# The opening of a two-layer trunk: c spread by products over 128 lines, factors by way of DRAM, a later half of weights and a sum in halves

## The chip, the cores and the metric

The kernel runs on one core of a Trainium2 chip. The metric is the device time of one execution, in microseconds (us); the time of a version is the median of its runs. A core has five engines with a queue of instructions each: TensorE (PE; its weight loads are shown apart as PEld), VectorE (DVE), ScalarE (ACT), GpSimd (POOL) and SyncE (SP), which here only issues DMAs. Each queue is worked off in order; an instruction waits until what it reads is there and the buffer that it writes is free. Transfers are moved by 16 DMA engines, whichever engine issues them. A "line" of a tile is one of its 128 partitions.

## The reference, cut to what matters

Two layers, 512 tokens of width 2048, all in float32. The modulation of a layer is three vectors of 2048 (shift, scale, gate), from a vector c. Layer 0 is a chunked retention, layer 1 a latent attention; the change lies in the opening of layer 0, up to its first projection.

```
c_act = silu(c)
for i in range(2):
    shift, scale, gate = split(c_act @ ada_w[i] + ada_b[i], 3)
    h = rmsnorm(x, norm_g[i]) * (1 + scale) + shift        # 512 x 2048
    proj = h @ w_in                                        # layer 0: q, k, v, gate
    y = retention(q, k, v) or attention(...)
    x = x + gate * (silu(g) * norm(y)) @ w_out
return rmsnorm(x, final_norm_g)
```

## The kernel before

Everything is kept transposed: features on the 128 lines, the 512 tokens along a line. The 2048 features are 16 blocks kt of 128; two blocks make a unit u. Each engine's order is the order of the program text: `queued(f)` puts what f issues behind whatever stands last on ACT, DVE, PE and SP; `behind(e)` does so for the engine named. No planner reorders it. Tiles of one tag share a fixed number of buffers, so a load into a recycled buffer waits for the last reader of the tile before.

A float32 product is made from two parts of each operand: a high part, rounded (a cast on ACT, L397), and the rest, the low part (a subtraction on DVE, L398 for weights, L485 for hT). Each product then takes three passes: high by high, one of the mixed ones ("early"), and the other mixed one ("late").

The opening runs like this:

- Loads on SP: x (eight parts), then in turn rows of ada_t ("aw(kt,s)", 1 MB each, s = 0 for shift, 1 for scale; `load_mod`, some in two halves) and 512 columns each of the first weights v, g and qk by units (`first_load`, 512 KB a unit). Four buffers hold aw, three the weights of later units.
- c comes as one line. Four products of one line of `ones` with it spread it to 128 lines in PSUM (`c_ps`), and ACT's silu writes it back as `c_all`. A transposition puts 48 rows of small vectors (biases, gains) into columns (`vec_ps`), which DVE copies to `vcol`.
- For each of the four blocks t of 128 tokens, ACT and DVE sum the squares of x, and POOL raises them to the power -1/2 (`x_r`, called `norm[t]` in the code). DVE (ACT for the last) multiplies the identity by it: `x_diag`. Products of x with the diagonal transpose and scale x at once into `xT_ps`; ACT copies them to `xT` (`keep_x`). Four more products of `ones` with the diagonals (`x_r` in PSUM) spread the factors to all lines, and DVE copies them to `x_factors`, with which the units u > 3, whose x^T is loaded later, are normalised on DVE (L716).
- POOL writes a line of `c_all` to DRAM (`c_d`) for later.
- The modulation of block kt: DVE multiplies aw(kt,s) by c_all and sums along the line (`sum_mod`, L425, one instruction of 2048 elements, or two of 1024). ACT makes the columns b_col and a_col of it (L453, L463), then hT_kt = a_col * xT + b_col as high part (L479), and again in full as h_3f or the like (L484), from which DVE makes the low part.
- PE takes, for each kt, the products of hT_kt with the weights v, g or qk that have a bank of PSUM at that time. For kt = 2 and 3 these are qk and g (the eight early passes of qk, its four late ones, then g), then v for u = 1, and so on. `prepare_ahead(2, low, ...)` writes the work of unit 2 between.

The names below: g_1 are the weights g of unit 1 (kt = 2, 3), whose two halves of 512 elements a line belong to kt = 2 and kt = 3; low hT_3 is the subtraction for hT_3 at L485; "sum (4,0)" is `sum_mod(4, 0)`.

Of the kernel before, what the change touches and what calls it, by code (L numbers as in the profile page):

```python
# [16 lines left out]
P = 128  # L17
# [32 lines left out]
def hybrid_trunk_kernel(  # L50
# [42 lines left out]
    o2_d = dram.tile([D, T], F32, name="o2_d")  # L93
    c_d = dram.tile([1, D], F32, name="c_d")

    def big(name, dt=F32R):
# [278 lines left out]
    def first_load(kind, u):  # L375

        cn = 512
        where = (("k4b", 4), ("k4b", 4)) if kind == "g" else None
        raw = big(f"{kind}0_{u}_raw", F32) if u == 0 else base.tile(
            [P, 2, cn], F32, tag="raw", bufs=3, name=f"{kind}0_{u}_raw"  # L380
        )
        src = w_first[u, "vgq".index(kind[0])]
        if u == 0:
            full[kind] = raw

        def load(*ki):
            if u < 4:
                nc.sync.dma_start(raw[:, ki[0]] if ki else raw, src[:, ki[0]] if ki else src)
            else:
                with behind(mybir.EngineType.Pool):  # L390
                    POOL.dma_start(raw, src)

        def prepare(*ki):
            if (kind, u) not in loaded:
                loaded[kind, u] = two_tiles(where, [P, 2, cn], f"{kind}0_{u}_p")
            hi, lo, w = (t[:, ki[0]] if ki else t for t in (*loaded[kind, u], raw))
            ACT.copy(hi, w)  # L397
            return lambda: DVE.tensor_sub(lo, w, hi.bitcast(F32))  # L398

        if kind == "qk" or u > 0:  # L400
            load()
        prepare.load = load
        return prepare

    def load_mod(kt, s):

        aw = l0p.tile([P, D], F32, tag="aw", bufs=4, name=f"aw_{kt}_{s}")
        n = 2 if kt < 2 or (kt, s) == (2, 0) else 1
        for j in range(n):
# [130 lines left out]
    def queued(fn, *args):  # L540
        with behind(A_, V_, T_, S_):
            return fn(*args)
# [77 lines left out]
    c_all = l0p.tile([P, D], F32, name="c_all")  # L620
    queued(ACT.dma_start, c_all[0:1, :], c)
    vrow = tmp("vec_rows", (P, P))
# [6 lines left out]
    for j, ps in enumerate(c_ps):  # L629
        queued(PE.matmul, ps, ones[0:1, :], c_all[0:1, j * T : (j + 1) * T], True, True)  # L630
        if j == 2:
            queued(PE.transpose, vec_ps[:, :N_OPEN], vrow[:N_OPEN, :], ident[:N_OPEN, :N_OPEN])

    def silu(j):
# [77 lines left out]

    factors = tmp("x_factors")

    def normalise(u):
        DVE.tensor_mul(xT[u], xT[u], factors.unsqueeze(1).to_broadcast([P, 2, T]))  # L716

    def load_unit(u):
# [11 lines left out]
        if u == 1:  # L730
            load_first("g", u)
        if u > 1:
            load_first(there, u)
        mods[2 * u + 1, 1] = queued(load_mod, 2 * u + 1, 1)
        if u == 1:
            load_first(there, u)
# [4 lines left out]
    def prepare_ahead(u, first=None, between=lambda: None):  # L741


        here, there = ("v", "qk") if u % 2 == 0 else ("qk", "v")
        low = queued(prepares[here, u])
        if u < 4:
            queued(first)
        queued(sum_mod, 2 * u, 0)
        if u > 3:
# [27 lines left out]
    for kt in (4, 5):  # L777
        keep_x(kt)
    x_r = acc("x_r")
    for t in range(NT):  # L780
        queued(PE.matmul, x_r[:, t * P : (t + 1) * P], ones, diags[t], True, True)
    queued(sum_mod, 0, 1, 0)
# [6 lines left out]
    queued(low_v)  # L789
    queued(DVE.tensor_copy, factors, x_r)  # L790
    queued(sum_mod, 1, 0, 0)
# [33 lines left out]
    queued(low)  # L825
    lows = [queued(prepares["g", 1], i) for i in range(2)]
    queued(lows[0])
    queued(sum_mod, 3, 1)
    low = make_first(3)
    queued(lows[1])  # L830
    queued(low)
    late[1] = queued(prepares["v", 1])
    queued(late[1])
    low = lambda: None
# [1954 lines left out]
```

## Time and profile before

| | |
|---|---|
| median of 3 runs | 2030.03 us (2029.43 to 2030.13) |
| the profiled execution | 2030.33 us |
| its span in the trace | 2028.5 us |
| TensorE busy | 2014.1 us, 99% of the span |
| VectorE busy | 1661.2 us, 82% |
| ScalarE busy | 1068.3 us, 53% |
| bytes moved by DMA | 462.44 MB, mean 228 GB/s |

The page's shares are means over the whole span; the change touches the first 62 us of it, so the parts that follow read the trace in stretches. Times of rows are in us from the start of the span. The names of tiles stand without their buffer numbers there: `aw<-aw,c_all` is a sum_mod, `g_p` a prepared g, `pair` a prepared tile of v or qk of the first units.

### The profile page before, as it was taken

The page shows a single profiled execution, that of the slowest core. Times are in us where ns is not written, and L with a number is a line of the kernel's source. Part 1 is how long each engine was busy: PE and PEld are TensorE (multiplying, and loading weights), DVE is VectorE, ACT ScalarE, POOL GpSimd, SP SyncE. Part 2 cuts the span into 40 slices and gives each one's busy share as a digit, 9 for nine tenths or more (in the row PEclk, how much of TensorE's full clock was granted, in tenths as well). Part 3 has the DMA queues.
Part 4 walks back from the last instruction along what each step waited for, and adds up shares of the span by engine and source line. Part 5 has one row for each costly group of instructions (what it writes and reads, how often), then busy time and mean ns, then how long its engine had stood idle before and what let it go on. Part 6 is the DMA issues. An engine that isn't in the chain of part 4 may idle for free.

```text
span 2028.5 us, 30162 instructions
## 1 busy us (share of the span) xinstructions
PE 2014.1 (99%) x11105; PEld 1806.9 (89%) x11105; DVE 1661.2 (82%) x2490; ACT 1068.3 (53%) x1697; POOL 109.7 (5%) x188
## 2 busy tenths in 40 slices
PE   9999999999999999999999999999999999999998
PEld 6888898989999888888888888899889999999888
DVE  7999888888989889776888788778978788886765
ACT  6777444544444544434444545445446676775444
POOL 0011010000000000000000000010001000000000
PEclk9999999999999999999999999999999999999999
DMA  9976787878787778765757576763467644446744
GB/s 386 416 304 228 237 281 234 286 229 276 253 268 262 240 248 296 264 207 188 248 177 263 181 252 212 272 203 108 165 198 217 198 145 150 124 149 221 240 151 142
DMA packets 225174, 462.44 MB, mean 228 GB/s; under 512 B 20785, under 2 KB 80241, under 8 KB 221569
## 3 DMA queue, kind: packets, MB, share of 16 engines
q1 hardware_dynamic: 210592, 414.25, 61.6%
q0 software_dynamic: 13632, 45.18, 5.7%
q8 instruction: 87, 1.43, 0.3%
q10 hardware_dynamic: 802, 1.08, 0.2%
q14 instruction: 61, 0.50, 0.1%
HBM read 417.44 MB, written 43.00 MB: 227 GB/s over the span
## 4 chain that ended last, share of the span: by engine, by line
PE 91%; DVE 5%; ACT 2%; issue 1%; DMA 1%; SPq 0%; DVEq 0%; POOL 0%; ACTq 0%; POOLq 0%
PE o L1614 14%; PE o L2618 4%; PE x L1000 2%; PE s L999 2%; PE y L999 2%; PE s L1001 2%; PE y L1000 2%; PE s L1000 2%; PE x L1001 2%; PE y L1001 2%; PE x L999 2%; PE x_qk L1100 2%; PE y_qk L1100 2%; PE s_qk L1100 2%; PE uv L2179 2%; PE qk L194 2%
## 5 line engine op out<-in xcount | busy, mean ns | idle before, releaser
L1614 PE MATMUL o<-o_h,o_p 128*128 128x512 f32 (+1 forms) x1088 | 311.7, 368 | 0.6 <-DVE o_p L138 0.6
L1614 PEld LDWEIGHTS o<-o_h,o_p 128*128 128x128 f32 x1088 | 201.0, 189 | 26.5 <-DVE o_p L138 1.0
L1614 PE MATMUL o<-o_l,o_p 128*128 128x512 f32 (+1 forms) x544 | 199.5, 367 | 0.0
L1614 PEld LDWEIGHTS o<-o_l,o_p 128*128 128x128 f32 x544 | 103.0, 189 | 12.5
L138 DVE TENSOR_TENSOR o_p<-o_r,o_p 128x1024 fp32r<-128x1024 f32 x64 | 78.1, 1223 | 25.7 <-ACT o_p L137 25.1
L2618 PE MATMUL o<-o_h,o_w 128*128 128x512 f32 (+1 forms) x336 | 79.8, 330 | 0.0
L1287 DVE SCALAR_TENSOR_TENSOR mod<-mod,c_odd 128x1024 f32<-128x1024 f32 x56 | 67.5, 1220 | 14.2 <-DMA mod<-in_ada_t_dram 14.1
L137 ACT CAST o_p<-o_r 128x1024 fp32r<-128x1024 f32 x64 | 66.3, 1048 | 22.9 <-PE o L1614 13.3
L425 DVE SCALAR_TENSOR_TENSOR aw<-aw,c_all 128x2048 f32<-128x2048 f32 (+1 forms) x37 | 73.0, 1998 | 1.3 <-DMA aw<-in_ada_t_dram 1.2
L192 PE MATMUL qk<-hT,qk_p 128*128 128x512 f32 x192 | 73.0, 380 | 0.0
L194 PE MATMUL qk<-hT,qk_p 128*128 128x512 f32 x192 | 72.9, 380 | 0.0
L193 PE MATMUL qk<-hT,qk_p 128*128 128x512 f32 x192 | 72.8, 379 | 0.0
L2618 PEld LDWEIGHTS o<-o_h,o_w 128*128 128x128 f32 x336 | 57.8, 190 | 4.7
L1458 ACT ACTIVATE yn<-y,nmr,gn_r 128x512 f32<-128x512 f32 x32 | 22.3, 776 | 65.3 <-DVE nmr L1452 65.3
L2618 PE MATMUL o<-o_l,o_w 128*128 128x512 f32 (+1 forms) x168 | 55.4, 329 | 0.0
L137 ACT CAST o_h<-o_in 128x1024 fp32r<-128x1024 f32 x24 | 25.1, 1048 | 56.8 <-PE o L193 41.0
L138 DVE TENSOR_TENSOR o_l<-o_in,o_h 128x1024 fp32r<-128x1024 f32 x24 | 29.3, 1222 | 27.2 <-ACT o_h L137 27.2
L1287 DVE SCALAR_TENSOR_TENSOR mod<-mod,c_bm 128x1024 f32<-128x1024 f32 x40 | 48.7, 1219 | 0.0
L193 PE MATMUL o<-o_l,o_w 128*128 128x512 f32 x128 | 48.5, 379 | 0.0
L194 PE MATMUL o<-o_h,o_w 128*128 128x512 f32 x128 | 48.5, 379 | 0.0
L192 PE MATMUL o<-o_h,o_w 128*128 128x512 f32 x128 | 48.5, 381 | 0.0
L138 DVE TENSOR_TENSOR o_w<-o_w_raw,o_w 128x1024 fp32r<-128x1024 f32 x32 | 38.8, 1219 | 8.3 <-ACT o_w L137 8.1
(1560 smaller groups left out, 6196.1 us busy)
## 6 DMA issues: line engine op xcount, KB each, us to landing
mod<-in_ada_t_dram SPq DMA_DIRECT2D x96, 512.0 KB, 6.0
o_r<-in_ret_w_out_dram SPq DMA_DIRECT2D x64, 512.0 KB, 5.3
aw<-in_ada_t_dram SPq DMA_DIRECT2D x27, 1024.0 KB, 9.0
mod_gate<-in_ada_t_dram SPq DMA_DIRECT2D x32, 512.0 KB, 5.0
o_w_raw<-in_mla_w_out_dram SPq DMA_DIRECT2D x32, 512.0 KB, 4.6
qk_r<-in_ret_w_in_dram SPq DMA_DIRECT2D x48, 256.0 KB, 3.5
qk_r<-qk_d SPq DMA_DIRECT2D x32, 256.0 KB, 5.9
v_r<-v_d SPq DMA_DIRECT2D x32, 256.0 KB, 5.2
```

The lines of the kernel that those rows point to most:

```text
L137: ACT.copy(hi, src)
L138: DVE.tensor_sub(lo, src, hi.bitcast(F32))
L192: PE.matmul(o, lhs[0], read(rhs[0]), start=first and not seeded, stop=False, skip_group_check=seeded)
L193: PE.matmul(o, lhs[0], read(rhs[1]), start=False, stop=False, skip_group_check=seeded)
L194: return PE.matmul(o, lhs[1], read(rhs[0]), start=False, stop=last, skip_group_check=seeded)
L999: PE.matmul(banks[b], a[0], paired(w[0]), start=first, stop=False, skip_group_check=True)
L1000: PE.matmul(banks[b], a[0], paired(w[1]), start=False, stop=False, skip_group_check=True)
L1001: PE.matmul(banks[b], a[1], paired(w[0]), start=False, stop=True, skip_group_check=True)
L1100: PE.matmul(o, w[wp][:, i, b * P : (b + 1) * P], paired(a[ap]), start=first and i + b + k == 0, stop=k == 2, skip_group_check=True,)
L1287: DVE.scalar_tensor_tensor(out=aw, in0=aw, scalar=1.0, in1=silu_c[j], op0=ALU.mult, op1=ALU.mult, accum_out=row_sums[piece][:, j, b : b + 1],)
L1614: PE.matmul(o, w[i][:, ki, c0 + b * P : c0 + (b + 1) * P], read(a[j]), start=first and i + j == 0, stop=last and i == 1, skip_group_check= ...
L2618: PE.matmul(banks2[b][:, cols], w[0][i][:, 0, b * P : (b + 1) * P], read(o2_moving(w, u, cols)[j]), start=u + i + j == 0, stop=u == KD - 1 ...
```

## The change

It has four parts, all in the opening.

1. c is loaded into line 127 of `c_all`; the other 127 lines are set to zero by DVE, and the four spreading products use all 128 lines of `ones`. Behind them and the transposition stand eight products of `ident` and `ones` into columns 128 to 255 of `vec_ps`, which nobody reads.
2. The factors: the four products into `x_r` and DVE's copy go. POOL writes each `norm[t]` to DRAM (`r_d`) and reads them back to all 128 lines of `x_factors`.
3. The weights g_1 are loaded in two halves, the second one behind aw(3,1), and its cast and its low part come behind h_3f and sum (3,1).
4. aw(4,0) is loaded and summed in halves; the first half stands ahead of low hT_3, the second behind the low part of v_1.

The head of TensorE's queue, before and after:

```order
L542 MATMUL c_ps_143<-c_all,ones 128x512
L542 MATMUL c_ps_144<-c_all,ones 128x512
L542 MATMUL vec_ps<-ident,vec_rows 128x48
L542 MATMUL c_ps_145<-c_all,ones 128x512
L542 MATMUL xT_ps_194<-x_diag_192,x_0_98 128x128
```

```order
L543 MATMUL c_ps_145<-c_all,ones 128x512
L543 MATMUL c_ps_146<-c_all,ones 128x512
L543 MATMUL vec_ps<-ident,vec_rows 128x48
L543 MATMUL c_ps_147<-c_all,ones 128x512
L543 MATMUL vec_ps<-ident,ones 128x128 x8
L543 MATMUL xT_ps_204<-x_diag_202,x_0_99 128x128
```

The eight products stand between the last c product and the first transposition. DVE's copy of `vec_ps` to `vcol` waits for the last instruction that writes the tile, now the eighth of them.

GpSimd's queue after its constants, before and after (`x_r<-x_v` is the root of a token block):

```order
L133 TENSOR_TENSOR x_r<-x_v,few 128x1 x2
L705 DMA c_d<-c_all 16x1x128
L133 TENSOR_TENSOR x_r<-x_v,few 128x1
L651 TENSOR_TENSOR x_r_238<-x_v_236,few 128x1
L391 DMA v_4_raw<-in_w_first_dram 128x1024
```

```order
L134 TENSOR_TENSOR x_r<-x_v,few 128x1
L709 DMA c_d<-c_all 16x1x128
L134 TENSOR_TENSOR x_r<-x_v,few 128x1
L720 DMA r_d<-x_r 128x1 x2
L134 TENSOR_TENSOR x_r<-x_v,few 128x1
L720 DMA r_d<-x_r 128x1
L655 TENSOR_TENSOR x_r_248<-x_v_246,few 128x1
L720 DMA r_d<-x_r_248 128x1
L722 DMA x_factors<-r_d 128x512
L392 DMA v_4_raw<-in_w_first_dram 128x1024
```

Five DMAs are new; two of them stand ahead of the third root.

VectorE around hT_3, before and after:

```order
L398 TENSOR_TENSOR g_1_p_415<-g_1_raw,g_1_p_414 128x512
L425 SCALAR_TENSOR_TENSOR aw_1_277,mc_1_419<-aw_1_277,c_all 128x2048
L398 TENSOR_TENSOR g_1_p_415<-g_1_raw,g_1_p_414 128x512
L485 TENSOR_TENSOR hT_423<-h_3f,hT_423 128x512
L398 TENSOR_TENSOR v_1_p<-v_1_raw,v_1_p 128x1024
L425 SCALAR_TENSOR_TENSOR aw_0_458,mc_0_472<-aw_0_458,c_all 128x2048
L398 TENSOR_TENSOR v_2_p<-v_2_raw,v_2_p 128x1024
```

```order
L399 TENSOR_TENSOR g_1_p_425<-g_1_raw,g_1_p_424 128x512
L426 SCALAR_TENSOR_TENSOR aw_1_292,mc_1_428<-aw_1_292,c_all 128x2048
L399 TENSOR_TENSOR g_1_p_425<-g_1_raw,g_1_p_424 128x512
L426 SCALAR_TENSOR_TENSOR aw_0_462,mc_0_477<-aw_0_462,c_all 128x1024
L486 TENSOR_TENSOR hT_432<-h_3f,hT_432 128x512
L399 TENSOR_TENSOR v_1_p<-v_1_raw,v_1_p 128x1024
L426 SCALAR_TENSOR_TENSOR aw_0_462,mc_0_477<-aw_0_462,c_all 128x1024
L432 TENSOR_TENSOR mc_0b<-mc_0_477 128x1
L399 TENSOR_TENSOR v_2_p<-v_2_raw,v_2_p 128x1024
```

The second g_1 low part stands where it stood, behind sum (3,1); between it and low hT_3 there is now the first half of sum (4,0), whose second half and the addition of the two follow v_1's low part.

ScalarE at the same place, before and after:

```order
L397 CAST g_1_p_414<-g_1_raw 128x512 x2
L453 ACTIVATE b_col_88<-mc_0_411,vcol 128x1
L463 ACTIVATE a_col_87<-mc_1_419,bias_152,vcol 128x1
L479 ACTIVATE hT_423<-xT_159,b_col_88,a_col_87 128x512
L484 ACTIVATE h_3f<-xT_159,b_col_88,a_col_87 128x512
L397 CAST v_1_p<-v_1_raw 128x1024
```

```order
L398 CAST g_1_p_424<-g_1_raw 128x512
L454 ACTIVATE b_col_89<-mc_0_421,vcol 128x1
L464 ACTIVATE a_col_88<-mc_1_428,bias_162,vcol 128x1
L480 ACTIVATE hT_432<-xT_169,b_col_89,a_col_88 128x512
L485 ACTIVATE h_3f<-xT_169,b_col_89,a_col_88 128x512
L398 CAST g_1_p_424<-g_1_raw 128x512
L398 CAST v_1_p<-v_1_raw 128x1024
```

The second of the two g_1 casts moved from ahead of b_col to behind h_3f; VectorE's second g_1 low part reads it. Elsewhere the order on each engine is that of before.

```diff
--- before.py
+++ after.py
@@ -92,6 +92,7 @@
     sg2_d = dram.tile([D, T], F32, name="sg2_d")
     o2_d = dram.tile([D, T], F32, name="o2_d")
     c_d = dram.tile([1, D], F32, name="c_d")
+    r_d = dram.tile([1, T], F32, name="r_d")
 
     def big(name, dt=F32R):
         return base.tile([P, 2, T], dt, tag="big", bufs=16, name=name)
@@ -397,7 +398,7 @@
             ACT.copy(hi, w)
             return lambda: DVE.tensor_sub(lo, w, hi.bitcast(F32))
 
-        if kind == "qk" or u > 0:
+        if kind == "qk" or u > 0 and (kind, u) != ("g", 1):
             load()
         prepare.load = load
         return prepare
@@ -405,7 +406,7 @@
     def load_mod(kt, s):
 
         aw = l0p.tile([P, D], F32, tag="aw", bufs=4, name=f"aw_{kt}_{s}")
-        n = 2 if kt < 2 or (kt, s) == (2, 0) else 1
+        n = 2 if kt < 2 or (kt, s) in ((2, 0), (4, 0)) else 1
         for j in range(n):
             cols = slice(j * D // n, (j + 1) * D // n)
             nc.sync.dma_start(aw[:, cols], ada_t[0, s * D + kt * P : s * D + (kt + 1) * P, cols])
@@ -618,7 +619,8 @@
 
 
     c_all = l0p.tile([P, D], F32, name="c_all")
-    queued(ACT.dma_start, c_all[0:1, :], c)
+    queued(DVE.memset, c_all[: P - 1, :], 0.0)
+    queued(ACT.dma_start, c_all[P - 1 :, :], c)
     vrow = tmp("vec_rows", (P, P))
     queued(ACT.dma_start, vrow[:32, :], ada_b[0, : 2 * D].rearrange("(r p) -> r p", p=P))
     queued(ACT.dma_start, vrow[32:N_OPEN, :], norm_g[0].rearrange("(r p) -> r p", p=P))
@@ -627,9 +629,11 @@
     c_ps = [acc(f"c_ps{j}") for j in range(4)]
     vec_ps = aux("vec_ps")
     for j, ps in enumerate(c_ps):
-        queued(PE.matmul, ps, ones[0:1, :], c_all[0:1, j * T : (j + 1) * T], True, True)
+        queued(PE.matmul, ps, ones, c_all[:, j * T : (j + 1) * T], True, True)
         if j == 2:
             queued(PE.transpose, vec_ps[:, :N_OPEN], vrow[:N_OPEN, :], ident[:N_OPEN, :N_OPEN])
+    for _ in range(8):
+        queued(PE.matmul, vec_ps[:, P : 2 * P], ones, ident, True, True)
 
     def silu(j):
         ACT.activation(c_all[:, j * T : (j + 1) * T], c_ps[j], AF.Silu)
@@ -711,6 +715,11 @@
         queued(ACT.copy, xT[kt // 2][:, kt % 2, :], xT_ps[kt])
 
     factors = tmp("x_factors")
+    with behind(mybir.EngineType.Pool):
+        for t in range(NT):
+            POOL.dma_start(r_d[0, t * P : (t + 1) * P], norm[t])
+    with behind(mybir.EngineType.Pool):
+        POOL.dma_start(factors, r_d[0].partition_broadcast(P))
 
     def normalise(u):
         DVE.tensor_mul(xT[u], xT[u], factors.unsqueeze(1).to_broadcast([P, 2, T]))
@@ -729,10 +738,13 @@
         mods[2 * u + 1, 0] = queued(load_mod, 2 * u + 1, 0)
         if u == 1:
             load_first("g", u)
+            queued(prepares["g", u].load, 0)
         if u > 1:
             load_first(there, u)
         mods[2 * u + 1, 1] = queued(load_mod, 2 * u + 1, 1)
         if u == 1:
+            queued(prepares["g", u].load, 1)
+        if u == 1:
             load_first(there, u)
 
     late = {}
@@ -742,10 +754,20 @@
 
 
         here, there = ("v", "qk") if u % 2 == 0 else ("qk", "v")
-        low = queued(prepares[here, u])
+        if u == 2:
+            queued(queued(prepares["g", 1], 1))
+        low = None if u == 2 else queued(prepares[here, u])
         if u < 4:
             queued(first)
-        queued(sum_mod, 2 * u, 0)
+        if u == 2:
+            queued(sum_mod, 2 * u, 0, 0)
+            queued(low3)
+            late[1] = queued(prepares["v", 1])
+            queued(late[1])
+            low = queued(prepares[here, u])
+            queued(sum_mod, 2 * u, 0, 1)
+        else:
+            queued(sum_mod, 2 * u, 0)
         if u > 3:
             queued(first)
             queued(late[u - 1])
@@ -776,9 +798,6 @@
     queued(make_shift, 0, shift0)
     for kt in (4, 5):
         keep_x(kt)
-    x_r = acc("x_r")
-    for t in range(NT):
-        queued(PE.matmul, x_r[:, t * P : (t + 1) * P], ones, diags[t], True, True)
     queued(sum_mod, 0, 1, 0)
     scale0 = scale_part(0)
     keep_x(6)
@@ -787,7 +806,6 @@
     queued(make_scale, 0, scale0)
     low = make_first(0, lambda: keep_x(7))
     queued(low_v)
-    queued(DVE.tensor_copy, factors, x_r)
     queued(sum_mod, 1, 0, 0)
     shift1 = shift_part(1)
     for kt in (1, 2, 3):
@@ -823,14 +841,9 @@
     low = make_first(2)
     queued(sum_mod, 3, 0)
     queued(low)
-    lows = [queued(prepares["g", 1], i) for i in range(2)]
-    queued(lows[0])
+    queued(queued(prepares["g", 1], 0))
     queued(sum_mod, 3, 1)
-    low = make_first(3)
-    queued(lows[1])
-    queued(low)
-    late[1] = queued(prepares["v", 1])
-    queued(late[1])
+    low3 = make_first(3)
     low = lambda: None
     queued(bank_products, "qk", 0)
     for u in range(1, NU):
```

## The prediction

> **What bounds the kernel now.** I read the page's busy times first, then the stretches of the opening, then the chain of waits from 38 to 66 us, then single rows. Columns of the stretches: from and to, length, busy time of PE, PEld, DVE, ACT and POOL with instruction counts, granted clock, DMA share, GB/s.
>
> ```profile
> PE 2014.1 (99%) x11105; PEld 1806.9 (89%) x11105; DVE 1661.2 (82%) x2490; ACT 1068.3 (53%) x1697; POOL 109.7 (5%) x188
> ...
> 0.00:30.00 30.00, 25.79 (x100) 17.15 (x101) 18.22 (x42) 19.02 (x39) 4.61 (x13) 1.00 0.96 364
> 30.00:62.00 32.00, 31.69 (x146) 27.04 (x145) 29.28 (x33) 22.14 (x38) 0.00 (x0) 1.00 1.02 415
> 62.00:130.00 68.00, 67.69 (x314) 59.21 (x314) 64.47 (x62) 51.98 (x85) 6.52 (x12) 1.00 1.01 414
> 130.00:2028.00 1898.00, 1888.93 (x10549) 1703.49 (x10547) 1549.18 (x2356) 975.18 (x1538) 98.52 (x163) 1.00 0.66 216
> ```
>
> TensorE is busy 99% of the span, and behind 62 us its order is the same in both programs; so what counts is how much earlier or later TensorE is at 62.4 us. Until 130 us the DMA engines have no room (share 1.01 to 1.04, 414 GB/s): a byte more ahead of a transfer delays it by its time at this rate.
>
> The chain of waits (start, length, what ran) shows who leads TensorE there:
>
> ```profile
> 42.77 2.22 DVE aw L425 x2
> ...
> 46.16 0.80 ACT h_3f L484
> ...
> 61.55 0.82 ACT hT L479
> ...
> 62.42 2.86 PE v L516 x12
> ```
>
> VectorE's modulation sums (aw), then the scalar engine's hT and h_3f, then TensorE. The sums depend on the loads of ada_t rows.
>
> **The opening, part by part.** Timeline rows: start, length, engine, line, instruction, count, and in brackets the idle time before and its releaser.
>
> ```profile
> 0.84 0.17 DVE L122 MEMSET ones<- 128x128 f32 x1 [0.84 <-PEq L2759]
> 0.95 0.06 DVE L125 MEMSET few<- 128x4 f32 x1
> 2.54 5.45 PE L542 MATMUL c_ps<-c_all,ones 1*128 1x512 f32 x6 [2.54 <-DMA c_all<-in_c_dram]
> 8.20 2.07 PE L542 MATMUL c_ps<-c_all,ones 1*128 1x512 f32 x2
> 8.30 0.21 DVE L542 COPY vcol<-vec_ps 128x48 f32<-128x48 f32 x1 [0.48 <-PE vec_ps L542]
> 9.32 1.23 DVE L653 SCALAR_TENSOR_TENSOR x_sq<-x 128x1024 f32<-128x1024 f32 x1 [0.60 <-DMA x<-in_x_dram]
> 11.26 10.35 PE L542 MATMUL xT_ps<-x_diag,x 128*128 128x128 f32 x64 [0.99 <-DVE x_diag L670]
> 11.89 1.22 DVE L653 SCALAR_TENSOR_TENSOR x_sq<-x 128x1024 f32<-128x1024 f32 x1 [0.69 <-DMA x<-in_x_dram]
> 12.70 2.77 PE L542 MATMUL xT_ps<-x_diag,x 128*128 128x128 f32 x12
> 14.26 0.29 DVE L670 TENSOR_SCALAR x_diag<-ident,x_r 128x128 f32<-128x128 f32 x1 [0.49 <-POOL x_r L133]
> 15.79 1.23 DVE L425 SCALAR_TENSOR_TENSOR aw<-aw,c_all 128x1024 f32<-128x1024 f32 x1 [1.24 <-DMA aw<-in_ada_t_dram]
> 18.43 1.50 PE L542 MATMUL xT_ps<-x_diag,x 128*128 128x128 f32 x12
> 23.18 2.06 PE L516 MATMUL v<-pair,hT 128*128 128x512 f32 x8 [0.68 <-ACT hT L479]
> ```
>
> *Memset of 127 lines.* 128 elements took 0.17 us, 4 took 0.06. Per element that is at most 0.17/128, for 2048 of them 2.7 us; at least (0.17-0.06)/124, 1.8 us. I take the middle, 2.2. It starts at about 1.0, so the c products, which before waited for c until 2.54, start at 3.2 (2.8 to 3.7). VectorE had nothing to do before its first square of x at about 6, so the memset holds up nothing else.
>
> *TensorE's pace.* Among twelve passes from 12.70 one takes about (2.77-0.42)/11 = 0.213 us, among those from 18.43 (1.50-0.27)/11 = 0.112 (the ends subtracted are those of the last pass, twice a pass and a bit): TensorE runs at half pace until some point between 15.5 and 18.4; I take 17.4, 6.2 us after the transposes began, though the granted clock reads 1.00 throughout. The 1-line c products, dense for 7.7 us, did not bring the full pace. By the same lag from 3.2 it would come at 9.4, if products with 128 lines count where those with one did not.
> The Trainium skill, "TensorE: Matmul & The Clock Gate", Part 1, has a shorter lag: the clock is halved until about 3.4 us of sustained activity, and nothing is said of lines. By it the full pace comes at 6.6; the 7.7 us of 1-line products that changed nothing do not agree with it.
>
> *Eight unused products.* They write the tile that VectorE's copy vcol<-vec_ps reads, so the copy, at 8.30 before, now waits for the last of them. The c products took 8.20-2.54 = 5.66 us to the last one's start, and that one two passes of some 0.85, in all 7.4 at half pace: from 3.2 to 10.6, or to 10.0 with full pace from 9.4. Eight products of two passes are 16 x 0.112 = 1.8, the end and the wake-up 0.3: the copy runs at 12.1, 3.8 later. (With full pace from 6.6: 8.6, and the copy at 10.7.) Behind it on VectorE stand the bias, two squares, three diagonals and then the sums. The idle times there, 0.60+0.69+0.49+1.24 = 3.0 us by the brackets, would take up the delay but for 0.8; the third of them, a wait for POOL's root, stays, since that root is now behind two DMA issues on POOL. So the sums start at 15.79+0.8+0.5 = 17.1, 1.3 later; with the copy at 10.7 at 15.8, as before, held by the same transfer.
>
> *Transposes.* They start behind the first diagonal, some 3 us later, and run at full pace: 64 x 0.112 = 7.2 us against 10.35. They end about where they did; the eight x_r passes behind them go, 0.9 us, but stood before a wait of 0.68 for hT_0 (the row at 23.18) and give little. hT_0 needs the four sums as well: v starts 0.4 later than 23.18 with sums at 17.1 (ScalarE's scale made them wait 0.9 before, which is taken up), and up to 1.3 earlier with sums at 15.8.
>
> *Factors by way of DRAM.* VectorE loses a copy (0.60 to the next start).
>
> ```profile
> 11.62 0.68 POOL L705 DMA_DIRECT2D c_d<-c_all  x1
> 23.30 0.68 DVE L542 COPY x_factors<-x_r 128x512 f32<-128x512 f32 x1
> 79.93 1.22 DVE L716 TENSOR_TENSOR xT<-xT,x_factors 128x1024 f32<-128x1024 f32 x1
> ```
>
> Five DMAs are issued on POOL, 0.68 us each by the c_d row; x_factors is first read at 79.93, so its way through DRAM is hidden by 50 us. POOL waits for the four writes before it issues the broadcast read; what is queued behind it there are loads of weights u = 4, far later, so nobody waits.
>
> **The decisive stretch, 38 to 50 us.** When may VectorE start sum (3,0), and who comes next?
>
> ```profile
> 26.90 0.33 SPq L411 DMA_DIRECT2D aw<-in_ada_t_dram  x1
> ...
> aw<-in_ada_t_dram SPq DMA_DIRECT2D x1, 1024.0 KB, 11.6
> ...
> 29.19 0.33 SPq L411 DMA_DIRECT2D aw<-in_ada_t_dram  x1
> ...
> aw<-in_ada_t_dram SPq DMA_DIRECT2D x1, 1024.0 KB, 13.1
> ...
> 7.00:9.00 2.00, 2.00 (x4) 0.67 (x3) 1.06 (x6) 0.97 (x2) 0.56 (x1) 1.00 0.99 384
> 9.00:11.00 2.00, 1.26 (x2) 0.00 (x0) 1.54 (x5) 1.36 (x4) 0.00 (x0) 1.00 1.03 424
> ...
> few<-const_rot_dram ACTq DMA_DIRECT2D x1, 2.0 KB, 7.0
> ```
>
> The load of aw(3,0) was issued at 26.90 and landed 11.6 us later, at 38.50; that of aw(3,1) landed at 29.19+13.1 = 42.29. VectorE started sum (3,0) at 39.27 (row below), only 0.77 us after its data. VectorE's own pace would start it at 39.27-0.60+0.4 = 39.07, or at 37.4 with the earlier front. And the transfers become later: the broadcast of x_factors writes 128 x 2 KB = 0.26 MB, 0.63 us at 414 GB/s. The four r_d writes are 512 single values of 4 bytes. Their nearest row is the load of the rotation constants, 128 lines of 16 bytes: while it was on its queue (issued at 2.1, landed 7.0 us later) the stretch to 9 us moved 384 GB/s, the next one 424, a loss of (424-384)/424 x 2.0 = 0.19 us. Each r_d write costs 0 to 0.19, all four 0 to 0.76; I take 0.3. The Trainium skill speaks against these writes ("DMA: Bandwidth & Descriptors", Specifications: transfers of under 512 B miss line rate and are done as read-modify-write); no row shows its price for 4 bytes. Sum: aw(3,0) lands at 38.50+0.63+0.3 = 39.43, and sum (3,0) starts 0.2 us later than before (by the ends -0.1 to +0.6). aw(3,1) has 256 KB less ahead (g's second half, 0.64 us) and lands at 42.29+0.93-0.64 = 42.58, ahead of its sum at 42.9. So whatever the front gains is spent waiting for the transfer: **+0.2**.
>
> Now the new order at hT_3.
>
> ```profile
> 39.27 2.29 DVE L425 SCALAR_TENSOR_TENSOR aw<-aw,c_all 128x2048 f32<-128x2048 f32 x1
> 40.61 0.61 ACT L397 CAST g_p<-g_raw 128x512 fp32r<-128x512 f32 x1
> 42.69 2.28 DVE L425 SCALAR_TENSOR_TENSOR aw<-aw,c_all 128x2048 f32<-128x2048 f32 x1
> 44.90 0.69 DVE L398 TENSOR_TENSOR g_p<-g_raw,g_p 128x512 fp32r<-128x512 f32 x1
> 45.44 0.82 ACT L479 ACTIVATE hT<-xT,b_col,a_col 128x512 fp32r<-128x512 f32 x1
> 46.30 2.86 PE L516 MATMUL qk<-hT,pair 128*128 128x512 f32 x12 [0.31 <-ACT hT L479]
> 46.99 0.69 DVE L485 TENSOR_TENSOR hT<-h_3f,hT 128x512 fp32r<-128x512 f32 x1 [1.41 <-ACT h_3f L484]
> 49.00 2.75 PE L516 MATMUL g<-hT,g_p 128*128 128x512 f32 x12
> ```
>
> Call hT_3's start s (45.44). Before, the cast and the low part of g's second half were done by then, h_3f ended at s+1.52, the low part of hT_3 stood first on VectorE (s+1.55 to s+2.24) and was ready long before TensorE, which wants it after eight of the twelve qk passes of the row at 46.30: 46.30 + 8 x 0.23 = 48.14, s+2.70. Now the cast stands behind h_3f (ends s+2.04), VectorE first waits for it (low g from s+2.08, 0.60 to the next start), then runs the first half of sum (4,0) (from s+2.68, 1.15), and only then the low part of hT_3: s+3.83 to s+4.52. TensorE goes on at s+4.57: 4.57-2.70 = **+1.87**, as a new wait in its queue, ahead of all g products.
>
> What comes back: TensorE also waited at 62.42 for hT_5, whose chain runs over VectorE: PE's v row at 62.42 stands at s+16.98, of which some 0.47 us is waiting (0.31 idle behind the g products and their end). In the new order hT_5 is ready some 0.9 later, s+17.9 (low g's 0.60 and VectorE's wait for the cast, 0.5, are new behind s, the halves and the add make 0.2, a wait of 0.3 behind low hT_3 goes), while TensorE arrives at s+16.98-0.47+1.87 = s+18.4. So this wait vanishes: **-0.47**.
>
> Of the rest: the second DMA issue for g and the one for aw(4,0) are 0.33 us each of SP's queue, which waits at those places for free buffers anyway; aw(4,0) by halves lets the first half sum start earlier, but hT_3's chain, not the transfer, sets its start. Nothing is counted for these.
>
> **Sum.** +0.2 +1.87 -0.47 = +1.6 us. The profiled run took 2030.33 us, span 2028.5, 0.3 above the median of the runs; on the median 2030.03 + 1.6 = 2031.6.
>
> **Rivals.** (a) *Ends on the other side: the transfers do not hold the sums.* If the loads of (3,0) and (3,1) land 1.9 us earlier than in my sum, and the full pace comes within the c products, sum (3,0) runs at VectorE's own pace, 37.4 to 37.6, d = -1.7, and the total is -1.7+1.40 = -0.3: 2029.7. Landing 1.0 earlier gives d = -0.85 and +0.5: 2030.5. For it: single transfers can land beside their place in the stream, since packets of several share the engines. Against it: the bytes ahead only grow. It decides for a faster kernel from d = -1.4. Chance 0.18.
> (b) *The pace does not rise early, and the copy blocks VectorE.* Then c ends at 10.6 and the unused products take 16 x 0.213 = 3.4: the copy at 14.3, 6.0 later, less 3.0 of idle: sums 3.0 or more later. hT_0 and all that follows on VectorE go with them, less the copy's 0.60: sum (3,0) up to 2.8 late, which with 1.40 is 4.2 (2034.2). If the transposes stay at half pace too, their 10.35 us from 14.5 bring hT_0 5.1 later: some 6.6 with the same slack taken off (2036.6). For it: the 7.7 us of 1-line products that did nothing. Chance 0.1.
> (c) *The 4-byte writes are dear*, 0.19 to 0.5 us each: every aw of this stretch is 0.5 to 1.7 later, total 2.1 to 3.3: 2032.1 to 2033.3. Chance 0.1.
> (d) The change does what I sum: 2031.0 to 2032.2, chance 0.62.
>
> **How the numbers follow.** A measurement of this kernel tells 0.2% (4.1 us) from no change. The time is that of (d). The range takes (d), (c) and most of (a): 2029.7 to 2033.4, leaving out (b) and some ends. Slower than 2034.1 is most of (b), 0.07; faster than 2026.0 is 0.02, which would need a gain that no row shows; within 0.2% the remaining 0.91.
>
> **What would show it.** Right: sum (3,0) starts at 39 to 40 us and its idle before names the transfer; a wait of near 1.9 us on TensorE between eight and the next qk passes at about 48.3, released by VectorE's low part of hT_3, with the first half of sum (4,0) just before it; no wait at hT_5; transposes at 0.11 us a pass from the first. Wrong: the wait at hT_3 under 1 us; VectorE idle nowhere before sum (3,0) with sums over a microsecond later or earlier; the vcol copy past 13 us; DMA under 400 GB/s from 14 to 22 us, which is (c).

## The result, and the profile after

The changed kernel takes 2042.34 us in the median of six runs (2041.41 to 2042.94), the kernel before beside it 2029.69 (2028.93 to 2030.13): slower by 12.65 us, ratio 1.0063 (95% interval 1.005 to 1.0076). I had forecast 2031.6, range 2029.7 to 2033.4. The profiled execution took 2042.85 us, span 2041.1.

The page's busy times after; TensorE works 2.8 us longer than before in a span that is 12.6 us longer:

```profile
PE 2016.9 (99%) x11113; PEld 1808.7 (89%) x11113; DVE 1662.3 (81%) x2493; ACT 1067.9 (52%) x1697; POOL 113.0 (6%) x193
```

The same four stretches as before, columns as there:

```profile
0.00:30.00 30.00, 19.74 (x95) 15.17 (x96) 13.14 (x32) 15.28 (x30) 7.80 (x17) 0.86 0.98 285
30.00:62.00 32.00, 27.70 (x104) 20.61 (x103) 24.61 (x34) 17.79 (x31) 0.55 (x1) 0.92 0.97 341
62.00:130.00 68.00, 68.00 (x317) 59.55 (x316) 64.22 (x64) 52.57 (x88) 5.30 (x10) 1.00 1.02 417
130.00:2028.00 1898.00, 1895.71 (x10554) 1707.94 (x10553) 1554.85 (x2357) 978.42 (x1544) 98.65 (x164) 1.00 0.66 217
```

The first two moved 285 and 341 GB/s where they had moved 364 and 415. The share of time in which the DMA engines are busy (next to last column) hardly changed: packets were under way all the time, and moved less. The share adds up the times of the packets, so it can pass 1. A narrower stretch shows where, 20 to 34 us, of before and then of after:

```profile
20.00:34.00 14.00, 13.32 (x61) 9.29 (x60) 11.32 (x20) 10.62 (x21) 0.00 (x0) 1.00 1.03 410
```

```profile
20.00:34.00 14.00, 9.26 (x38) 6.58 (x38) 6.09 (x12) 6.56 (x14) 0.01 (x1) 0.76 1.09 164
```

A share of 1.09, at 164 GB/s. The transfers new in this time are the four writes of the factors, 0.5 KB each. Their rows in the list of DMA issues (the first three with their median to landing, then the last):

```profile
r_d<-x_r POOLq DMA_DIRECT2D x3, 0.5 KB, 11.3
...
r_d<-x_r POOLq DMA_DIRECT2D x1, 0.5 KB, 14.3
```

POOL's timeline, the first two writes, the last, and the read behind them:

```profile
15.21 1.13 POOL L720 DMA_DIRECT2D r_d<-x_r  x2
...
19.09 0.58 POOL L720 DMA_DIRECT2D r_d<-x_r  x1 [0.30 <-POOL x_r L655]
33.99 0.55 POOL L722 DMA_DIRECT2D x_factors<-r_d  x1 [14.31 <-DMA r_d<-x_r]
```

2 KB in all took from 15.21 to 19.09+14.3 = 33.4 us. From 14 to 20 us the engines still moved 402 GB/s; from there until the last write had landed, every other load crawled. The chain of waits says the same:

```profile
8.45 8.59 DMA aw<-in_ada_t_dram
...
17.05 19.46 DMA aw<-in_ada_t_dram
...
36.58 12.95 DMA aw<-in_ada_t_dram
...
57.24 0.52 ACT g_p L398
...
58.39 1.23 DVE aw L426 x2
59.61 0.62 DVE hT L486
60.23 0.04 issue
60.27 1.13 PE qk L517 x4
```

Before, VectorE's sums led the chain; now loads of ada_t do until 49.5 us. Then comes the stretch at hT_3, with the low part behind the half sum. Timeline rows of the steps that the prediction spoke of:

```profile
1.40 1.76 DVE L543 MEMSET c_all<- 127x2048 f32 x1 [0.38 <-issue]
3.22 5.17 PE L543 MATMUL c_ps<-c_all,ones 128*128 128x512 f32 x6 [3.22 <-DVE c_all L543]
8.51 1.12 PE L543 MATMUL c_ps<-c_all,ones 128*128 128x512 f32 x2
11.46 0.21 DVE L543 COPY vcol<-vec_ps 128x48 f32<-128x48 f32 x1 [3.71 <-PE vec_ps L543]
13.72 9.04 PE L543 MATMUL xT_ps<-x_diag,x 128*128 128x128 f32 x64 [2.30 <-DVE x_diag L674]
17.15 1.22 DVE L426 SCALAR_TENSOR_TENSOR aw<-aw,c_all 128x1024 f32<-128x1024 f32 x1
27.50 3.78 PE L517 MATMUL v<-pair,hT 128*128 128x512 f32 x8 [4.74 <-ACT hT L480]
49.54 2.29 DVE L426 SCALAR_TENSOR_TENSOR aw<-aw,c_all 128x2048 f32<-128x2048 f32 x1 [0.20 <-DMA aw<-in_ada_t_dram]
55.72 0.81 ACT L480 ACTIVATE hT<-xT,b_col,a_col 128x512 fp32r<-128x512 f32 x1
57.78 0.69 DVE L399 TENSOR_TENSOR g_p<-g_raw,g_p 128x512 fp32r<-128x512 f32 x1 [2.52 <-ACT g_p L398]
58.39 1.22 DVE L426 SCALAR_TENSOR_TENSOR aw<-aw,c_all 128x1024 f32<-128x1024 f32 x1
59.53 0.69 DVE L486 TENSOR_TENSOR hT<-h_3f,hT 128x512 fp32r<-128x512 f32 x1
60.27 1.13 PE L517 MATMUL qk<-hT,pair 128*128 128x512 f32 x4 [1.69 <-DVE hT L486]
```

The books: hT_3 starts at 55.72 instead of 45.44, 10.28 later. The new wait at the late qk passes and the one that goes at hT_5 make 1.4 by the prediction's steps, in all 11.68. Comparing like instructions on VectorE in the two traces, the shift is 11.67 at 125 us and still 11.7 at 770. A further 1.1 comes between 770 and 785 us, at waits for prepared weights of another stage; the last kernel below, which is not late there, has it as well. I did not follow it.

### The profile page after: what moved, and what is told of

Its sections match the earlier page's. It is cut to its first block, busy times and chain, and to the rows that moved or that the text cites. A ratio compares the mean times of both kernels' runs of the same rounds, so it can differ in the third digit from the quotient of the medians.

```text
span 2041.1 us, 30189 instructions
## 1 busy us (share of the span) xinstructions
PE 2016.9 (99%) x11113; PEld 1808.7 (89%) x11113; DVE 1662.3 (81%) x2493; ACT 1067.9 (52%) x1697; POOL 113.0 (6%) x193
## 3 DMA queue, kind: packets, MB, share of 16 engines
q0 software_dynamic: 13840, 45.44, 5.7%
## 4 chain that ended last, share of the span: by engine, by line
PE 91%; DVE 4%; DMA 3%; ACT 1%; issue 1%; SPq 0%; POOL 0%; DVEq 0%; ACTq 0%; POOLq 0%
PE o L1627 16%; PE o L2631 4%; PE x L1013 2%; PE y L1014 2%; PE x L1014 2%; PE y L1012 2%; PE y L1013 2%; PE s L1014 2%; PE x L1012 2%; PE s L1012 2%; PE s L1013 2%; PE x_qk L1113 2%; PE uv L2192 2%; PE y_qk L1113 2%; PE s_qk L1113 2%; PE qk L195 2%
## 5 line engine op out<-in xcount | busy, mean ns | idle before, releaser
L1627 PEld LDWEIGHTS o<-o_l,o_p 128*128 128x128 f32 x544 | 103.0, 189 | 12.6
```

The source lines that it names most:

```text
L1627: PE.matmul(o, w[i][:, ki, c0 + b * P : c0 + (b + 1) * P], read(a[j]), start=first and i + j == 0, stop=last and i == 1, skip_group_check= ...
```

## The experiments

Two theories at first. **W**: the four writes of single values hold up the loads. **C**: the copy of vec_ps behind the eight products, and TensorE's pace falling back while it waits. The order at hT_3 is a third step, with a number of its own. The edits are to the kernel before unless the text says otherwise. Differences are to the kernel before, run beside each.

| kernel | median us | to before | ratio, 95% interval |
|---|---|---|---|
| a_products | 2032.35 | +2.35 | 1.0011 (1.0002 to 1.002) |
| b_dram | 2040.64 | +10.64 | 1.005 (1.0036 to 1.0063) |
| c_order | 2030.72 | +0.72 | 1.0003 (0.9995 to 1.0012) |
| d_c | 2030.86 | +0.86 | 1.0005 (0.9996 to 1.0014) |
| w_one | 2035.81 | +5.66 | 1.0028 (1.0018 to 1.0039) |
| w_act | 2036.45 | +6.30 | 1.0032 (1.002 to 1.0044) |
| w_apart | 2029.83 | -0.32 | 1.0 (0.999 to 1.0009) |
| w_rows | 2030.40 | +0.25 | 1.0 (0.999 to 1.001) |
| w_64 | 2030.08 | -0.01 | 0.9999 (0.999 to 1.0008) |
| w_16 | 2030.01 | -0.08 | 1.0 (0.9991 to 1.0009) |
| w_p16 | 2030.59 | +0.20 | 1.0001 (0.9991 to 1.001) |
| w_p8 | 2034.57 | +4.18 | 1.002 (1.0011 to 1.0029) |
| d_mend | 2030.00 | -0.09 | 1.0001 (0.9992 to 1.001) |
| c_low3 | 2030.25 | +0.16 | 1.0001 (0.9992 to 1.001) |
| all_mend | 2030.95 | +0.56 | 1.0003 (0.9993 to 1.0013) |

### Which part costs the time

**a_products**, the changed kernel without the way through DRAM:

```diff
...
-            POOL.dma_start(r_d[0, t * P : (t + 1) * P], norm[t])
...
-        POOL.dma_start(factors, r_d[0].partition_broadcast(P))
...
+    x_r = acc("x_r")
+    for t in range(NT):
+        queued(PE.matmul, x_r[:, t * P : (t + 1) * P], ones, diags[t], True, True)
...
+    queued(DVE.tensor_copy, factors, x_r)
```

> The changed kernel with the factors spread by products and copied as before, no writes to DRAM and no broadcast read. Theory W (the four writes of single 4-byte values hold up every load from 20 to 34 us): the loads go back to over 400 GB/s in 20 to 34 us, sum (3,0) starts at 38.5 to 39.5, and only the new order at hT_3 is left, +1.4 on before: 2030.5 to 2031.5 us. Rival C (the copy of vec_ps behind the eight products, and TensorE's pace falling back in its idle time): the delay stays for the most part, 2036 to 2042 us.

Its loads from 20 to 34 us, then sum (3,0) and TensorE's late qk passes of hT_3 in the timeline:

```profile
20.00:34.00 14.00, 13.32 (x61) 9.31 (x60) 11.74 (x22) 10.62 (x21) 0.00 (x0) 1.00 1.03 410
```

```profile
39.38 2.28 DVE L425 SCALAR_TENSOR_TENSOR aw<-aw,c_all 128x2048 f32<-128x2048 f32 x1
...
50.11 1.13 PE L516 MATMUL qk<-hT,pair 128*128 128x512 f32 x4 [1.70 <-DVE hT L485]
```

The loads are back at 410 GB/s, 10 of the 12.65 us are gone, and the wait at hT_3 is left. The median, 2.35 over before, is 0.9 above W's range. In the profiled execution (2031.60 us) like instructions are 1.50 late at 200 us, near the 1.4 of the prediction's steps.

**b_dram**, only the way through DRAM:

```diff
...
+        for t in range(NT):
+            POOL.dma_start(r_d[0, t * P : (t + 1) * P], norm[t])
...
+        POOL.dma_start(factors, r_d[0].partition_broadcast(P))
...
-        queued(PE.matmul, x_r[:, t * P : (t + 1) * P], ones, diags[t], True, True)
...
-    queued(DVE.tensor_copy, factors, x_r)
```

> The kernel before with only the factors sent by way of DRAM (the four writes, the broadcast read; the x_r products and the copy gone). Theory W: aw(3,0) lands some 10 us later, 2038 to 2041 us. Rival C: 2029 to 2030.5 us, as before.

```profile
20.00:34.00 14.00, 5.81 (x17) 3.70 (x15) 3.94 (x8) 4.58 (x10) 0.00 (x0) 0.76 0.95 147
```

```profile
34.23 0.55 POOL L719 DMA_DIRECT2D x_factors<-r_d  x1 [15.87 <-DMA r_d<-x_r]
```

147 GB/s and +10.64 us, with one-line c products, no unused ones, and the old order. W stands; C falls as the main cause. The broadcast read is not issued before 34.23 us; by then (410-147)/410 x 14 = 9.0 us of the stream were lost, so the writes account for most of the 10.64. What the read adds was not run by itself: from 34 to 38 us the rate is 251 GB/s where it was 415, and loads that start late stand there beside the read.

**c_order**, only the later half of g_1 and sum (4,0) in halves:

```diff
...
+            queued(queued(prepares["g", 1], 1))
...
+            queued(sum_mod, 2 * u, 0, 0)
+            queued(low3)
+            late[1] = queued(prepares["v", 1])
+            queued(late[1])
+            low = queued(prepares[here, u])
+            queued(sum_mod, 2 * u, 0, 1)
...
```

> The kernel before with only g_1's second half later and sum (4,0) in halves. By the prediction's sum a wait of 1.87 us at the late qk passes of hT_3 and the end of the wait at hT_5: +1.4, 2031.1 us. Rival: the 256 KB less ahead of aw(3,1) start hT_3 earlier by 0.3 or more and the total is under +1.0.

VectorE's and TensorE's rows:

```profile
47.19 0.69 DVE L398 TENSOR_TENSOR g_p<-g_raw,g_p 128x512 fp32r<-128x512 f32 x1 [2.52 <-ACT g_p L397]
47.80 1.22 DVE L425 SCALAR_TENSOR_TENSOR aw<-aw,c_all 128x1024 f32<-128x1024 f32 x1
48.94 0.69 DVE L485 TENSOR_TENSOR hT<-h_3f,hT 128x512 fp32r<-128x512 f32 x1
...
49.69 1.13 PE L516 MATMUL qk<-hT,pair 128*128 128x512 f32 x4 [1.69 <-DVE hT L485]
```

The late qk passes start 1.86 us later than the passes before allow (1.69 idle and the end of a pass), hT_5's wait is gone, and hT_3 itself comes 0.3 earlier: the shift of like instructions is +1.09 at 200 us. The median says +0.72; the interval cannot tell it from nothing; the traces, of one execution each, show the step.

**d_c**, only c by 128 lines with the eight unused products:

```diff
-    queued(ACT.dma_start, c_all[0:1, :], c)
+    queued(DVE.memset, c_all[: P - 1, :], 0.0)
+    queued(ACT.dma_start, c_all[P - 1 :, :], c)
...
-        queued(PE.matmul, ps, ones[0:1, :], c_all[0:1, j * T : (j + 1) * T], True, True)
+        queued(PE.matmul, ps, ones, c_all[:, j * T : (j + 1) * T], True, True)
...
+    for _ in range(8):
+        queued(PE.matmul, vec_ps[:, P : 2 * P], ones, ident, True, True)
```

> The kernel before with only c spread by products with 128 lines and the eight unused products behind. Theory W: transfers set sum (3,0), at 38.5 to 39.3 us as before, so 2029.0 to 2029.9 us. Rival C: the copy of vec_ps at 11.5 instead of 8.3 us and the pace falling back delay hT_0 by 1 us and more, and the kernel ends 1 to 5 us later, 2031 to 2035 us.

Rows of its timeline and of its stretch from 14 to 20 us:

```profile
13.59 9.04 PE L542 MATMUL xT_ps<-x_diag,x 128*128 128x128 f32 x64 [2.30 <-DVE x_diag L673]
...
40.29 2.28 DVE L425 SCALAR_TENSOR_TENSOR aw<-aw,c_all 128x2048 f32<-128x2048 f32 x1
```

```profile
14.00:20.00 6.00, 6.00 (x41) 6.00 (x40) 5.41 (x13) 2.92 (x9) 3.26 (x3) 0.72 1.03 405
```

Between the theories' numbers. TensorE waits 2.30 us for the first diagonal, since VectorE's copy waited for the unused products; the granted clock falls to 0.72 in that stretch, and the transposes take 9.04 us where a_products, with the clock at 1.00, took 7.52. Sum (3,0) starts at 40.29 instead of 39.27, and like instructions are 1.02 later at 400 us. So C is real, but worth one microsecond. Taken singly, W is 10.6, the order 0.7 by the median and 1.1 by the trace, and C up to 1; in the changed kernel, whose sums wait for loads until 49.5 us, C may be hidden.

The 0.9 of a_products above W's range stays open. Its TensorE has the same idle time as d_c's, and in the profiled execution the granted clock stayed at 1.00 from 14 to 20 us. A pace lost in its other runs does not explain it, as far as their mean clocks tell: six of the eleven runs show a mean clock of 0.998, as d_c's profiled one does, and the median of these six is 2032.4 us, that of the five at 0.999 is 2032.3.

### What makes the writes dear

Two theories: **N**, neighbouring values hold each other up; **S**, every small write is dear, wherever it goes.

**w_one**, one of the four writes, read by nobody, the factors by products:

```diff
...
+        POOL.dma_start(r_d[0, :P], norm[0])
```

> The kernel before (factors by products) with one additional write of 128 neighbouring 4-byte values to DRAM on POOL's queue, behind the first root; nobody reads it. If each write costs the loads the same: a quarter of the 10.6 us of all four, +2 to +3.5, 2032 to 2033.5 us. If the cost comes of several such writes under way together: under +1, at most 2031 us.

```profile
20.00:34.00 14.00, 7.95 (x30) 5.64 (x29) 7.97 (x15) 7.81 (x17) 0.00 (x0) 0.76 0.89 252
```

More than the first expectation: 512 bytes cost 5.66 us, (410-252)/410 x 14 = 5.4 us of the stream. The prices of several do not simply add up.

**w_act**, four writes on ScalarE's queue instead of POOL's:

```diff
...
+    for t in range(NT):
+        queued(ACT.dma_start, r_d[0, t * P : (t + 1) * P], norm[t])
```

> The kernel before with the same four additional writes of 128 neighbouring 4-byte values, issued by ScalarE behind the last diagonal instead of by POOL. Theories N and S: as dear as on POOL's queue, +8 to +12, 2038 to 2042 us. If POOL's queue is the cause: +0.5 to +2 (four issues on ScalarE), 2030.5 to 2032 us.

```profile
20.00:34.00 14.00, 10.13 (x35) 5.68 (x35) 6.92 (x13) 6.44 (x15) 0.00 (x0) 0.88 0.90 191
```

+6.30 lies between the two expectations: under the 8 of N and S, far over the 2 that were to be left if POOL's queue were the cause. The writes are dear without that queue. They cost less than the 10.6 of b_dram, which has the read as well and starts its writes 3 us earlier; whether the queue has a part in that difference is not shown.

**w_apart**, each value in a DRAM row of its own, 512 bytes apart, and **w_rows**, as many pieces of 512 bytes (the names behind # tell which run has the line):

```diff
+    r_d = dram.tile([T, P], F32, name="r_d")
...
+            POOL.dma_start(r_d[t * P : (t + 1) * P, 0:1], norm[t])     # w_apart
+            POOL.dma_start(r_d[t * P : (t + 1) * P, :], diags[t])      # w_rows
```

> The kernel before with four additional writes of 128 values of 4 bytes, each value in a DRAM row of its own, 512 bytes apart. Theory N (the cost comes of neighbouring values that share a stretch of DRAM, written one after the other): under +1.5, 2030 to 2031.5 us, loads over 390 GB/s from 20 to 34 us. Theory S (the cost is that of small writes, wherever they go): +8 to +11, 2038 to 2041 us.

> The kernel before with four additional writes of 128 rows of 512 bytes (the diagonals) to DRAM on POOL's queue: as many pieces as the four writes of single values, 128 times the bytes. Theories N and S: 0.26 MB more in the stream, +0.3 to +0.8, 2030.3 to 2030.8 us. If the number of pieces on POOL's queue or its waits cost the time, +8 to +11.

The stretch of w_apart and that of w_rows:

```profile
20.00:34.00 14.00, 13.32 (x58) 9.22 (x57) 12.08 (x22) 10.77 (x22) 0.00 (x0) 1.00 1.03 410
```

```profile
20.00:34.00 14.00, 13.33 (x60) 9.29 (x59) 11.86 (x20) 10.61 (x21) 0.00 (x0) 1.00 1.03 409
```

Theory N: 512 separate 4-byte pieces cost nothing that the runs can tell when they lie 512 bytes apart. Not the size, not the number of pieces, but their being neighbours. The Trainium skill ("DMA: Bandwidth & Descriptors", Specifications) puts a line at 512 bytes, below which a transfer is done as read-modify-write; these rows do not agree that size alone costs, whatever it does inside.

**w_64**, **w_p16**, **w_p8**: the four writes with 64, 16 and 8 bytes from value to value; **w_16**: one write of 128 neighbouring pieces of 16 bytes.

```diff
+    r_d = dram.tile([T, 16], F32, name="r_d")   # w_64; [T, 4] in w_p16, [T, 2] in w_p8
...
+            POOL.dma_start(r_d[t * P : (t + 1) * P, 0:1], norm[t])
...
+        POOL.dma_start(r_d, vcol[:, :NT])        # w_16, r_d of [P, NT]
```

> The kernel before with four additional writes of 128 values of 4 bytes, 64 bytes apart in DRAM (512 bytes apart cost nothing, 4 bytes apart 10.6 us with the read). If only values that share 64 bytes hold each other up: 2029.5 to 2031 us. If the stretch they must not share is longer: 2032 to 2041 us.

> The kernel before with one additional write of 128 neighbouring pieces of 16 bytes (four columns of vcol) on POOL's queue, 2 KB in all. If the cost goes by the pieces under way in one stretch, 512 bytes of DRAM hold 32 of them and not 128 as with 4 bytes: +1 to +3 where one write of 4-byte values cost 5.7, 2031 to 2033 us. If every small neighbouring piece costs the same: +5 to +6, 2035 to 2036.5 us.

> The kernel before with four additional writes of 128 values of 4 bytes, 16 bytes apart: as many pieces in 64 bytes (four) as with the pieces of 16 bytes, which cost nothing, but each smaller than that. If it is the number of pieces that share a stretch of DRAM: 2029.5 to 2031 us. If a piece of 4 bytes whose neighbour lies within 64 bytes is what costs: 2035 to 2041 us.

> The kernel before with four additional writes of 128 values of 4 bytes, 8 bytes apart (eight in 64 bytes, half as many as in the changed kernel). If the number of pieces in a stretch sets the cost and it starts above four: +2 to +7, 2032 to 2037 us. If only values that touch each other cost: 2029.5 to 2031 us.

The stretch of w_p16 and that of w_p8:

```profile
20.00:34.00 14.00, 12.03 (x50) 8.13 (x49) 11.72 (x20) 9.97 (x20) 0.00 (x0) 1.00 1.06 384
```

```profile
20.00:34.00 14.00, 10.52 (x35) 6.11 (x34) 9.43 (x17) 8.49 (x19) 0.00 (x0) 0.88 0.94 287
```

A row of doses: 4 bytes apart 147 GB/s (with the broadcast read behind) and +10.6 us, 8 bytes 287 and +4.2, 16 bytes 384 and +0.2, 64 and 512 bytes nothing. At the same distance of 16 bytes neither four writes of 4-byte pieces (w_p16) nor one of 16-byte pieces (w_16) changes the time; w_p16 still loses (410-384)/410 x 14 = 0.9 us of the stream. So the price goes by how close the pieces lie or, which is the same in these runs, by how many of them fall on one small stretch of DRAM: it starts between four and eight in 64 bytes. Whether 64 bytes is the length that counts, and which part of the memory path makes the pieces wait, is not shown.

### The two smaller faults mended

**d_mend**, d_c with the unused products in the tile of the first transposition, which PE itself writes next:

```diff
...
-        queued(PE.matmul, vec_ps[:, P : 2 * P], ones, ident, True, True)
+        queued(PE.matmul, xT_ps_0[:, :P], ones, ident, True, True)
...
```

> The kernel before with c spread by products with 128 lines, and the eight unused products written to the tile of the first transposition instead of to vec_ps, so that the copy to vcol waits only for the transposition of the vectors. Theory: the copy runs at 8.4 to 9.0 us, TensorE is idle under 0.5 us ahead of the transposes and keeps its pace, and sum (3,0) starts 0 to 0.7 us earlier than before: 2029.3 to 2030.0 us; against the same change with the copy held, 0.5 to 1.5 less. Rival (the copy is not what cost there): 2030.5 to 2031.5 us.

```profile
9.04 0.21 DVE L542 COPY vcol<-vec_ps 128x48 f32<-128x48 f32 x1 [1.31 <-PE vec_ps L542]
...
11.69 1.95 PE L542 MATMUL xT_ps<-x_diag,x 128*128 128x128 f32 x16
```

The copy runs at 9.04, the first 16 transposing passes follow the unused products without a wait and at 0.112 us a pass, and the qk passes of hT_3 start at 45.69 us, 0.6 before those of the kernel before. The time is that of before: 0.6 us is under what the runs tell. Against d_c, each set against the kernel before, it is 0.95 us less (-0.09 and +0.86), and like instructions at 400 us stand 1.6 earlier (-0.61 and +1.02).

**c_low3**, c_order with low hT_3 ahead:

```diff
...
-            queued(queued(prepares["g", 1], 1))
+            low_g = queued(prepares["g", 1], 1)
+            queued(low3)
+            queued(low_g)
...
             queued(sum_mod, 2 * u, 0, 0)
-            queued(low3)
```

> The kernel before with g_1's second half later and sum (4,0) in halves, but low hT_3 first on VectorE behind h_3f, ahead of the second low g_1 and of the half sum. By the prediction's step the wait of 1.86 us at the late qk passes goes; hT_5 comes some 0.9 later than before against a wait of 0.47 there: net +0.3 to +0.9 on before less the 0.3 that hT_3 gains by the earlier transfers, 2029.9 to 2030.7 us, and no wait over 0.3 us on TensorE between hT_3's early and late qk passes. Rival: the wait has another cause (the later cast or load) and stays over 1 us.

```profile
45.47 2.86 PE L516 MATMUL qk<-hT,pair 128*128 128x512 f32 x12 [0.36 <-ACT hT L479]
...
62.14 2.86 PE L516 MATMUL v<-v_p,hT 128*128 128x512 f32 x12 [0.84 <-ACT hT L479]
```

All twelve qk passes of hT_3 run in one piece: the wait is gone, by the order on VectorE alone. What returns is a longer wait at hT_5, 0.84 where it was 0.31.

**all_mend**, the three together (factors by products):

> The whole change with its three faults mended: factors by products and copied, unused products into the tile of the first transposition, low hT_3 first on VectorE. By the steps: hT_3 0.3 to 0.6 us earlier, hT_5's wait about 1 us instead of 0.47, so 2029.5 to 2030.3 us, not to be told from before.

2030.95, 0.65 over the range, not to be told from before (1.0003, 0.9993 to 1.0013). Like instructions stand 0.28 earlier than in the kernel before from 200 to 600 us, as the steps say; the wait at 770 to 785 us, here 1.3 us, takes it back. No version beat the kernel before by more than the runs can tell.

## Why the prediction was wrong, point by point

- *"Each r_d write costs 0 to 0.19"*: this term failed, and it alone explains the miss: without the way through DRAM the kernel takes 2032.35 us (a_products), inside my range. I had 0.3 us for all four writes; they took 9.0 us of the stream before the broadcast read was issued, and writes and read together 10.6 us of the time (b_dram). Rival (c) had the right place and sign, with 0.5 us a write as its dearest price; one write alone cost 5.7. What the prediction named as its mark came as well: 328 GB/s from 14 to 22 us, under 400. The row I called nearest, the load of the rotation constants, is small pieces as well, but it writes to 128 lines of the core's memory; the new transfers write neighbouring words of DRAM. No row of before had that, so the upper end of the bound was not an upper end. The one sentence that spoke against the writes, from the Trainium skill ("DMA: Bandwidth & Descriptors", Specifications), pointed at the right operation. Its ground, transfers under 512 bytes, is not by itself what the runs show: w_apart writes 4 bytes at a time and costs nothing.
- *"+1.87" at hT_3 and "-0.47" at hT_5*: right to a few hundredths. The late qk passes of the changed kernel start 4.55 us after hT_3 (60.27-55.72; forecast 4.57), the excess is 1.86 there and in c_order, and no wait is left at hT_5.
- *"+0.2", the front's gain spent waiting for the transfer*: the mechanism is wrong without the writes too. In a_products sum (3,0) starts at 39.38, 0.1 later than before, near the forecast, but no wait for a transfer stands ahead of it; in d_c VectorE's own pace has it start at 40.29, one microsecond late. That the figure was near in a_products is luck.
- *Memset and copy*: products from 3.22 (forecast 3.2); the memset's row has 1.76 us behind 0.38 us of idle time that the profile puts to no wait, 2.1 together (forecast 2.2); the copy at 11.46 (12.1); the sums at 17.15 (17.1).
- *TensorE's full pace within c's products*: right, at c's sixth pass, near 8 us (forecast 9.4); the 16 unused passes from 9.47 took 1.95 us, 0.112 a pass. So the first condition of rival (b) did not hold.
- *Transposes at full pace*: missed. I saw that they would start 3 us later and did not ask what 2.3 us of idle time does to the pace just gained: from about 14.8 to 18.1 us the passes took 0.21 us each, and all 64 took 9.04 us (forecast 7.2).
- *v's first product at 23.6*: 27.50, since ScalarE waited for v's weights; without the writes 24.19 (d_c).

## What to carry to other kernels

Don't write single 4-byte values side by side to DRAM while the DMA engines are needed: put them at least 16 bytes apart, or collect them into pieces of 16 bytes first (both were run here, beside loads of some 410 GB/s). A busy DMA share with few GB/s is the sign to look for a tiny transfer that takes ten microseconds to land. When no row shows an operation, ask whether the nearest row goes in the same direction to the same memory before its price is used as a bound; and before unused work is put into a tile, look who reads that tile, and what waits behind him.

## What the runs showed of the hardware that was not expected

- 512 bytes written as 128 neighbouring 4-byte values held the 16 DMA engines back for 5.4 us of their stream (w_one, 252 instead of 410 GB/s from 20 to 34 us). Four such writes held them back from ScalarE's queue (191 GB/s) as well as from POOL's (147 in b_dram). With 16 bytes from value to value, four writes left 384 GB/s and the time as it was.
- TensorE's half pace ended some 3 to 6 us after dense 128-line passes began, not always at the same time: c's first six passes took 5.46 us in d_mend, nearly all at half pace, 4.78 in d_c and 4.31 in all_mend, the last ones at full pace. Passes with one line, 7.7 us of them in the kernel before, ended it in none of the kernels here. The half pace came back after 2.30 us without work in the changed kernel and in d_c (granted clock 0.72 from 14 to 20 us), but not in the profiled execution of a_products (1.00). The Trainium skill, "TensorE: Matmul & The Clock Gate", Part 1, speaks of a free-running window, by which the same program may fall on either side; that the times vary agrees with this. On products with one line that part says nothing.
